# Sample-state and retention stages of a hybrid decoder layer: deeper buffers, operations between engines, another spread of matmul products

## The chip, the core and the metric

The kernel runs on one core of a Trainium2 chip. The engines are called as the profile calls them: PE (matrix multiply; PEld is its weight load), DVE (VectorE), ACT (ScalarE), POOL (GpSimd), SP (SyncE, which here issues only DMAs). POOL issues DMAs too, beside its own arithmetic. The metric is the device time of one launch in microseconds (us). The kernel before took 1690.91 us, the median of three runs from 1685.97 to 1693.16.

## The reference, cut to what matters

One inference step of a one-layer decoder for a prompt of 1024 positions and 8 sample sequences of 4 positions (32 columns), so 1056 columns go through each projection:

```python
xn = rms_norm(x, g_pre_mix); h = xn @ w_in           # 1024 -> 5888 columns
q_a, k_a, v_a, q_r, k_r, v_r, gate_r, gm_a, gm_r = split(h)
o_a = sliding-window attention(q_a, k_a, v_a)         # 8 heads, 128 wide window
# retention, 4 heads, key 128, value 256, chunks of 128 (prompt) or 4 (sample):
scores = (q @ k.T) * dmask;  inner = scores @ v
cross  = (q @ s0) * q_decay
s_new  = gamma**L * s0 + (k * k_decay).T @ v
o_r = head_rms(inner + cross)
mixed = (sigmoid(gm_a) * (o_a @ w_a) + sigmoid(gm_r) * ((silu(gate_r) * o_r) @ w_r)) @ w_o
x = x + rms_norm(mixed);  x = x + rms_norm(conv_ffn(rms_norm(x)))
```

For the samples, `s0` is an input of 8 sequences x 4 heads x 128 x 256 numbers, and `s_new` is an output of the same size.

## The kernel before, in words

**Precision.** A matrix is held as two fp32r tiles, a high part (an ACT copy that rounds) and a low part (source minus high, usually on DVE). The helper `split(hi, lo, src, eng=None)` does both, the low on `eng` or, by default, on DVE. A multiply is three matmuls (lines 255, 256, 257). The helper `ew` (lines 223 and 225) records every elementwise operation: on DVE as a SCALAR_TENSOR_TENSOR at line 223, on POOL as a TENSOR_TENSOR at line 225. So the tiles, not the line, tell such operations apart.

**Products.** Large projections use seven products in place of eight for a 2x2 block multiply. One product is 4 x 3 = 12 matmuls of 128x264. `in_split` loads the raw weights of one pair of 128-column groups of `w_in` (1 MB, two DMAs on SP), forms four sums of 128x512 on DVE and splits seven operands (`w_split`: ACT copy, DVE low). `stream()` is a generator that runs the 16 pairs of this stage, in the order of the list `ORDER`; each of its `yield`s stands behind one product. `adv(n)` runs n products. Pairs 0 to 3 are the retention q and k of heads 0 to 3, pairs 4 to 7 the output gates, 8 to 15 the merge gates. A finished pair is handed to a `post` function: `post_qk` applies the rotary (per half of the columns and per q or k: a DVE shuffle, a POOL multiply by `rcos`, a DVE multiply of `sh` by `rsin`, a POOL add of `sh`; tiles 128x528), `post_gate` a Silu on ACT, `post_ga` a Sigmoid on ACT and a DVE multiply by a tile `zt` that SP loads from `gm_d`.

**Sample stage** (about 298 to 448 us of the profile). `adv(18)` runs, then `for h in range(4): for _ in sample(h): adv(3)`. `sample(h)` prepares a head, then goes in four steps over the eight sequences, two at a time: SP loads their states (`s0`, 128x512, line 1018), `split` makes `s0s` from them, four matmuls with 64 rows add `q @ s0` into `po` (line 1024), two masked keys `kb` are made on DVE (line 1028), two matmuls form `k.T @ v` in `pk` (line 1030), DVE updates `s0` from `pk` (line 1031), and POOL issues its store to `ret_sample` (line 1033). After the head and after each step three products follow in the program.

**Block stage** (about 448 to 704 us). 32 blocks, four heads of eight. `front` makes scores and splits, `middle` the matmuls and the running state (line 1134), `tail` the normalised output times the gate. Per block `adv(2)`, `middle`, `adv(1)`, `tail`, `adv(1)`. `loads(g + 1)` brings the next block: q and k for two blocks at a time (line 1079, SP), v per block (line 1081, POOL). In the tails of blocks 0, 1 and 2 of each head weight sums are made for later stages: `quad_sums` loads two quarters of `w_r` or `w_down` into a `zt` tile (two buffers), four DVE operations follow and a store. `z_sums` in blocks 4 and 7, and `post_ga`, use the same two `zt` buffers. After the last tail the remaining products of the stream run, then the multiply by `w_r` begins (its matmuls write `ps_m`) and with it the merge, until about 840 us.

**What sets the order.** The framework orders the instructions of every engine itself, by a simulated timeline; an engine then runs its list strictly in that order, and each instruction waits in front of its engine for its inputs and for its output buffer. Pools give a name so many buffers (`bufs`); a tile that is asked for when all are taken waits until the oldest is released. PE's accumulators `ps_a` have two buffers in these stages.

## Time and profile before

| what | value |
|---|---|
| runs | 1685.97, 1690.91, 1693.16 us |
| profiled execution, device time | 1688.03 us |
| its span (first to last instruction) | 1686.2 us |
| outside the span | 1.8 us |
| mean granted clock of PE | 0.996 |
| busy in the span: PE, DVE, ACT, POOL | 1629.5, 1269.6, 868.4, 500.9 us |

Busy time counts instructions on the engine; DMA issues are not in it. A wait is put down to the operation whose semaphore came last. A row of grouped instructions gives the busy time of all, the mean of one in ns, and the idle time of the engine just before them with what ended it. A row of a window table gives the length, then for PE, PEld, DVE, ACT and POOL the busy time and, in brackets, the number of instructions, then the granted clock of PE, the busy share of the DMA engines and GB/s.

### The profile page before, as it was taken

What the parts mean: (1) busy time and instruction counts of PE and PEld (TensorE: products, weight loads), DVE (VectorE), ACT (ScalarE), POOL (GpSimd) and SP (SyncE); (2) the same over time, 40 slices, a digit from 0 to 9 for tenths busy, and PEclk for the clock granted to TensorE, in tenths of its full rate; (3) what the DMA queues carried; (4) which work ended last, traced back from release to release, by engine and by line L of the source; (5) the groups of instructions that cost most, each with busy time, mean ns of one, the idle gap of its engine ahead of it and who ended that gap; (6) DMA issues with size and microseconds to landing.
All of it is one profiled execution on the core that took longest, in us unless ns stands there. A gap on an engine that the chain in (4) does not pass through costs nothing.

```text
span 1686.2 us, 32968 instructions
## 1 busy us (share of the span) xinstructions
PE 1629.5 (97%) x12643; PEld 1588.5 (94%) x12643; DVE 1269.6 (75%) x2227; ACT 868.4 (51%) x1942; POOL 500.9 (30%) x714
## 2 busy tenths in 40 slices
PE   8999999888999989999999999999999999999997
PEld 7999989888999989999778999999999999999997
DVE  7887737799586677658757888888888888445476
ACT  6566534434566655564433555555555556444343
POOL 4232420455253443331412122212213323111111
PEclk9999999999999999999999999999999999999999
DMA  7312222445686677596722144454444447866664
GB/s 198 66 45 73 80 65 103 135 130 171 205 256 202 213 252 227 183 298 213 234 94 72 60 145 159 148 163 148 149 146 146 146 151 252 257 182 202 194 184 149
DMA packets 268944, 273.92 MB, mean 162 GB/s; under 512 B 22785, under 2 KB 229921, under 8 KB 268770
## 3 DMA queue, kind: packets, MB, share of 16 engines
q1 hardware_dynamic: 235025, 155.25, 31.7%
q0 software_dynamic: 33760, 116.57, 20.0%
q8 instruction: 99, 1.62, 0.4%
q14 instruction: 60, 0.48, 0.1%
HBM read 184.24 MB, written 87.49 MB: 161 GB/s over the span
## 4 chain that ended last, share of the span: by engine, by line
PE 68%; DVE 11%; DMA 9%; issue 7%; ACT 3%; POOL 1%; SPq 1%; DVEq 0%; POOLq 0%; ACTq 0%
PE ps_m L255 9%; PE ps_m L257 9%; PE ps_m L256 9%; PE ps_t L256 8%; PE ps_t L255 7%; PE ps_t L257 7%; PE ps_mm L255 3%; PE ps_mm L256 3%; PE ps_mm L257 3%; PE ps_q L255 2%; PE ps_q L257 2%; PE ps_q L256 2%; DMA a_in<-a_d 1%; DVE w L223 1%; DVE w_lo L223 1%
## 5 line engine op out<-in xcount | busy, mean ns | idle before, releaser
L255 PE MATMUL ps_q<-xh,w 128*128 128x264 f32 x512 | 148.6, 291 | 7.5 <-DVE pair L925 5.1
L223 DVE SCALAR_TENSOR_TENSOR w_lo<-w_raw,w_hi 128x1024 fp32r<-128x1024 f32 x83 | 104.2, 1261 | 66.0 <-ACT w_hi L228 59.0
L255 PE MATMUL ps_t<-xh,w_hi 128*128 128x264 f32 (+2 forms) x524 | 148.9, 284 | 0.0
L256 PE MATMUL ps_t<-xl,w_hi 128*128 128x264 f32 (+2 forms) x524 | 148.7, 284 | 0.0
L257 PE MATMUL ps_t<-xh,w_lo 128*128 128x264 f32 (+2 forms) x524 | 148.0, 283 | 0.0
L257 PE MATMUL ps_m<-xh,w_lo 128*128 128x264 f32 x512 | 145.6, 285 | 1.2 <-DVE w_lo L223 1.2
L255 PE MATMUL ps_m<-xh,w_hi 128*128 128x264 f32 x512 | 145.9, 285 | 0.2 <-ACT w_hi L228 0.2
L256 PE MATMUL ps_m<-xl,w_hi 128*128 128x264 f32 x512 | 145.5, 284 | 0.0
L256 PE MATMUL ps_q<-xl,w 128*128 128x264 f32 x512 | 145.4, 284 | 0.0
L257 PE MATMUL ps_q<-xh,w 128*128 128x264 f32 x512 | 145.3, 285 | 0.0
L223 DVE SCALAR_TENSOR_TENSOR w<-w_raw,w 128x512 fp32r<-128x512 f32 x152 | 106.0, 701 | 26.1 <-ACT w L329 25.7
L1458 DVE SCALAR_TENSOR_TENSOR c_out<-u_ext,fconst,c_out 128x1024 f32<-128x1024 f32 x96 | 121.8, 1279 | 2.6 <-ACT c_out L1454 0.5
L228 ACT CAST w_hi<-w_raw 128x1024 fp32r<-128x1024 f32 x62 | 65.2, 1052 | 107.1 <-PE ps_t L256 75.3
L329 ACT CAST w<-w_raw 128x512 fp32r<-128x512 f32 x152 | 94.2, 622 | 40.4 <-DVE w_raw L223 25.0
L255 PEld LDWEIGHTS ps_q<-xh,w 128*128 128x128 f32 x512 | 96.3, 188 | 10.0 <-DVE pair L925 7.0
L257 PEld LDWEIGHTS ps_t<-xh,w_lo 128*128 128x128 f32 x524 | 98.7, 188 | 0.0
L256 PEld LDWEIGHTS ps_t<-xl,w_hi 128*128 128x128 f32 x524 | 98.6, 188 | 0.0
L255 PEld LDWEIGHTS ps_t<-xh,w_hi 128*128 128x128 f32 x524 | 98.6, 188 | 0.0
L257 PEld LDWEIGHTS ps_m<-xh,w_lo 128*128 128x128 f32 x512 | 96.3, 188 | 1.7 <-DVE w_lo L223 1.7
L255 PEld LDWEIGHTS ps_m<-xh,w_hi 128*128 128x128 f32 x512 | 96.3, 188 | 0.4 <-ACT w_hi L228 0.4
L256 PEld LDWEIGHTS ps_q<-xl,w 128*128 128x128 f32 x512 | 96.4, 188 | 0.0
L256 PEld LDWEIGHTS ps_m<-xl,w_hi 128*128 128x128 f32 x512 | 96.2, 188 | 0.0
(468 smaller groups left out, 6204.9 us busy)
## 6 DMA issues: line engine op xcount, KB each, us to landing
w_raw<-in_w_up SPq DMA_DIRECT2D x48, 512.0 KB, 4.2
w_raw<-in_w_in SPq DMA_DIRECT2D x42, 512.0 KB, 4.3
w_raw<-s_d SPq DMA_DIRECT2D x60, 256.0 KB, 3.9
t_d<-t POOLq DMA_DIRECT2D x24, 528.0 KB, 4.0
t<-t_d POOLq DMA_DIRECT2D x24, 528.0 KB, 5.1
t<-in_w_down SPq DMA_DIRECT2D x40, 256.0 KB, 4.7
s_d<-t POOLq DMA_DIRECT2D x20, 512.0 KB, 3.8
w_raw<-in_w_down SPq DMA_DIRECT2D x36, 256.0 KB, 4.8
```

The lines of the kernel that those rows point to most:

```text
L223: pinned(V.scalar_tensor_tensor(out=out, in0=in0, scalar=1.0, in1=in1, op0=mult, op1=op))
L228: pinned(S.copy(out=hi, in_=src))
L255: TE.matmul(ps, wh, xh, start=start, stop=False, **kw)
L256: TE.matmul(ps, wh, xl, start=False, stop=False, **kw)
L257: TE.matmul(ps, wl, xh, start=False, stop=stop, **kw)
L329: S.copy(out=t[:, 0:4], in_=src)
L1458: V.scalar_tensor_tensor(out=c[:, NS:], in0=u[:, g, NU + t:NU + t + SEQ], scalar=sc[t], in1=c[:, NS:], op0=mult, op1=add)
```

## The change

- `sample`: the state loads go through `load_s0`, with four buffers in place of two, and are issued two steps ahead (the first two before `adv(18)`). The masked keys `kb` are made by ACT (`S.mul`) and not by DVE. The low part of `s0s` is made by POOL and not by DVE. `r8` and the sample's `o` have one buffer in place of two, and `os8` shares the buffer of `t8`.
- Four products, not three, follow each head start and each step (`adv(4)`).
- Blocks: `qk` is loaded for one block at a time into three buffers, `vt` has four buffers in place of three, both two blocks ahead. The products per block alternate between 3 and 4 (`adv(g % 2)`).
- The weight sums are made in the tails of blocks 0, 2 and 6, no longer 0, 1 and 2.
- `in_split`: the second sum is written over the first (`s1`). `ORDER` puts gate 0 ahead of the q and k of head 3, and the first two merge-gate pairs (8 and 9) one place later.

```diff
-    ORDER = [0, 1, 2, 3, 4, 5, 8, 6, 9, 7, 10, 11, 12, 13, 14, 15]
+    ORDER = [0, 1, 2, 4, 3, 5, 6, 8, 7, 9, 10, 11, 12, 13, 14, 15]
...
-        s1, s2 = [wx["sum"].tile([P, 4, P], F32, name="s%d" % q) for q in range(2)]
+        s1 = wx["sum"].tile([P, 4, P], F32, name="s1")
         yield w_split(a11, V)
         ew(V, s1, a21, a22, add)
         yield w_split(s1, V)
-        ew(V, s2, s1, a11, sub)
-        yield w_split(s2, V)
+        ew(V, s1, s1, a11, sub)
+        yield w_split(s1, V)
         yield w_split(a12, V)
-        ew(V, a12, a12, s2, sub)
+        ew(V, a12, a12, s1, sub)
...
+    s0s_ = {}
+
+    def load_s0(n):
+        if n >= 2 * DB:
+            return
+        h, bb = n // 4, 2 * (n % 4)
+        s0s_[n] = ST("s0", (P, 2, 256), bufs=4)
+        ld.dma_start(out=s0s_[n], in_=I["state_ret"][0, bb:bb + 2, h].rearrange("b k e -> k b e"))
...
-        r8 = ST("r8", (P, 2, P), bufs=2)
+        r8 = ST("r8", (P, 2, P))
...
-            s0 = ST("s0", (P, 2, 256), bufs=2)
-            ld.dma_start(out=s0, in_=I["state_ret"][0, bb:bb + 2, h].rearrange("b k e -> k b e"))
+            s0 = s0s_[(h * DB + bb) // 2]
+            load_s0((h * DB + bb) // 2 + 2)
             s0s = ST("s0s", (P, 2, 2, 256), F32R)
-            split(s0s[:, 0], s0s[:, 1], s0)
+            split(s0s[:, 0], s0s[:, 1], s0, G)
...
-                V.tensor_scalar(out=kb, in0=f32(h8)[:, 1], scalar1=bm[:, bb + b:bb + b + 1],
-                                scalar2=None, op0=mult)
+                S.mul(kb, f32(h8)[:, 1], bm[:, bb + b:bb + b + 1])
...
-        os8 = ST("o", (P, 256), bufs=2)[:NS]
+        os8 = ST("t8", (P, 256))[:NS]
...
+    for n in range(2):
+        load_s0(n)
     adv(18)
     for h in range(4):
         for _ in sample(h):
-            adv(3)
+            adv(4)
...
-    def loads(g):
+    def load_qk(g):
...
-        if tt % 2 == 0:
-            qks[g // 2] = qk2 = ST("qk2", (P, 2, 2 * P), bufs=2)
-            c = NS + P * tt
-            ld.dma_start(out=qk2, in_=qk_d[h].rearrange("i p t -> p i t")[:, :, c:c + 2 * P])
-        vts[g] = ST("vt", (P, 2, 256), F32R, bufs=3)
+        qks[g] = ST("qk", (P, 2, P), bufs=3)
+        ld.dma_start(out=qks[g], in_=qk_d[h].rearrange("i p t -> p i t")[:, :, cols(tt)])
+
+    def load_v(g):
...
+        vts[g] = ST("vt", (P, 2, 256), F32R, bufs=4)
         st.dma_start(out=f32(vts[g][:, 1]), in_=v_d[h, tt])
...
-        if tt < 3:
+        if tt in (0, 2, 6):
             q_ = quarters(ST("zt", (P, T), bufs=2))
-            down_sums(20 + h, q_) if tt == 2 else quad_sums(w_r, r_d, h, 0, tt, q_)
+            down_sums(20 + h, q_) if tt == 6 else quad_sums(w_r, r_d, h, 0, tt // 2, q_)
...
-        loads(g + 1)
+        load_qk(g + 2)
+        load_v(g + 2)
...
         adv(2)
         m = middle(g, *f)
-        adv(1)
+        adv(g % 2)
...
-    adv(len(ORDER) * 14 - 8 - 78 - 4 * NBLK - 1)
+    adv(len(ORDER) * 14 - 8 - 98 - 7 * NBLK // 2 - 1)
```

Two places show how the lists of the engines move. First POOL, in a stretch of sample steps while the rotary of a q and k pair runs (`pair<-pair,rcos` and `pair<-pair,sh` are the rotary; `out_ret_sample` is the store of a step's states; `rs` a reciprocal root). Before:

```order
L225 TENSOR_TENSOR pair<-pair,rcos 128x528
L225 TENSOR_TENSOR pair<-pair,sh 128x528
L1033 DMA out_ret_sample<-s_4346 128x2x256
L826 DMA qk_d<-pair 128x2x528
L225 TENSOR_TENSOR pair<-pair,rcos 128x528
L1033 DMA out_ret_sample<-s_4421 128x2x256
L225 TENSOR_TENSOR pair<-pair,sh 128x528
```

and in the change, over as many steps:

```order
L225 TENSOR_TENSOR s0s<-s_4249,s0s 128x512
L225 TENSOR_TENSOR pair<-pair,sh 128x528
L1037 DMA out_ret_sample<-s_4168 128x2x256
L225 TENSOR_TENSOR pair<-pair,rcos 128x528
L225 TENSOR_TENSOR pair<-pair,sh 128x528
L225 TENSOR_TENSOR s0s<-s_4454,s0s 128x512
L1037 DMA out_ret_sample<-s_4249 128x2x256
L826 DMA qk_d<-pair 128x2x528
```

The lows of the states now stand between the rotary's operations on POOL, one per step, ahead of that step's store.

The second place is DVE in steps of the same kind (`kb` the masked keys, `w` and `w_raw` weights of the products, `s` followed by a number the states or a weight sum, `sh` the rotary). Before:

```order
L1028 TENSOR_SCALAR kb<-h_4656,bm 128x128
L1031 SCALAR_TENSOR_TENSOR s_4715<-s_4715,ps_a 128x512
L1028 TENSOR_SCALAR kb<-h_4656,bm 128x128
L223 SCALAR_TENSOR_TENSOR s0s<-s_4794,s0s 128x512
L223 SCALAR_TENSOR_TENSOR w_4774<-w_raw,w_4774 128x512
L925 TENSOR_TENSOR pair<-ps_q_4664,pair 128x264
L223 SCALAR_TENSOR_TENSOR w_raw<-w_raw,s_4680 128x512
L822 STREAM_SHUFFLE sh<-pair 128x528
```

In the change:

```order
L223 SCALAR_TENSOR_TENSOR sh<-sh,rsin 128x528
L1035 SCALAR_TENSOR_TENSOR s_4168<-s_4168,ps_a 128x512
L223 SCALAR_TENSOR_TENSOR w7x<-w_raw,w7x 128x512
L822 STREAM_SHUFFLE sh<-pair 128x528
L223 SCALAR_TENSOR_TENSOR sh<-sh,rsin 128x528
L1035 SCALAR_TENSOR_TENSOR s_4249<-s_4249,ps_a 128x512
L223 SCALAR_TENSOR_TENSOR s_4603<-w_raw 128x512
```

Between two state updates (line 1031, now 1035) DVE no longer has the masked keys and the low of the states, and has what the products and the rotary need.

More of the change, by code (lines that the diff above doesn't have):

```diff
@@ L852, in trunk @@
     pairs += [(GM0 + m * P, GM0 + m * P + P, post_gm(m)) for m in range(0, KD, 2)]
-    def in_ahead(n):
-        ws = pair_split(pair_weights(w_in, *pairs[n][:2]))
-        return itertools.chain([next(ws) for _ in range(NPRE)], ws)
-    ORDER = [0, 1, 2, 3, 4, 5, 8, 6, 9, 7, 10, 11, 12, 13, 14, 15]
+    ORDER = [0, 1, 2, 4, 3, 5, 6, 8, 7, 9, 10, 11, 12, 13, 14, 15]
     PEND = []
@@ L969, in rep, with finish @@
         return a.rearrange("p (o t) -> p o t", o=1).broadcast_to([P, 4, NS])
-    def finish(po, n, s, h):
+    def finish(po, n, s, h, bufs=2):
         ssq = sml.tile([P, 1], F32, name="ss")[:n]
-        o = ST("o", (P, 256), bufs=2)[:n]
+        o = ST("o", (P, 256), bufs=bufs)[:n]
         S.activation(o, po[:n, :256], AF.Square, accum_out=ssq)
@@ L1034, in sample @@
             yield
-        os8 = ST("o", (P, 256), bufs=2)[:NS]
+        os8 = ST("t8", (P, 256))[:NS]
         S.copy(out=os8, in_=po[NS:2 * NS])
         V.tensor_tensor(out=os8, in0=po[0:NS], in1=os8, op=add)
-        S.copy(out=z8[:, h], in_=turn(pt, finish(os8, NS, 1, h)))
+        S.copy(out=z8[:, h], in_=turn(pt, finish(os8, NS, 1, h, 1)))
+    for n in range(2):
+        load_s0(n)
     adv(18)
@@ L1075, in loads @@
         h, tt = divmod(g, NB)
[L1076 to L1080 removed]
+        qks[g] = ST("qk", (P, 2, P), bufs=3)
+        ld.dma_start(out=qks[g], in_=qk_d[h].rearrange("i p t -> p i t")[:, :, cols(tt)])
+    def load_v(g):
+        if g >= NBLK:
+            return
+        h, tt = divmod(g, NB)
+        vts[g] = ST("vt", (P, 2, 256), F32R, bufs=4)
         st.dma_start(out=f32(vts[g][:, 1]), in_=v_d[h, tt])
@@ L1099, in front @@
         h, tt = divmod(g, NB)
-        q, k = (qks[g // 2][:, i, P * (tt % 2):P * (tt % 2) + P] for i in range(2))
+        q, k = (qks[g][:, i] for i in range(2))
         vt = vts[g]
@@ L1187, in ahead @@
             state["dm"] = mask(g // NB)
-        loads(g + 1)
+        load_qk(g + 2)
+        load_v(g + 2)
         return front(g, state["dm"])
-    loads(0)
+    for g in range(2):
+        load_qk(g)
+        load_v(g)
     coming, behind = ahead(0), None
```

2 lines of the change are left out of this document (1 added, 1 removed).

## The prediction

> **What bounds the kernel now.** I read the page's busy shares first, then a table of windows by stage, then the waits of PE in the two stages that the change touches, and last single instructions.
>
> ```profile
> PE 1629.5 (97%) x12643; PEld 1588.5 (94%) x12643; DVE 1269.6 (75%) x2227; ACT 868.4 (51%) x1942; POOL 500.9 (30%) x714
> 298.00:424.00 126.00, 108.65 (x839) 103.98 (x839) 116.74 (x195) 51.97 (x134) 67.86 (x57) 0.99 0.47 148
> 424.00:448.00 24.00, 21.10 (x172) 20.50 (x171) 13.22 (x28) 10.90 (x24) 4.38 (x6) 1.00 0.61 194
> 448.00:729.00 281.00, 270.44 (x2189) 266.39 (x2190) 201.35 (x509) 168.38 (x459) 116.66 (x190) 0.99 0.71 226
> 729.00:840.00 111.00, 107.84 (x781) 101.23 (x781) 84.85 (x125) 56.00 (x99) 38.00 (x28) 1.00 0.78 240
> 940.00:1200.00 260.00, 260.00 (x2141) 260.00 (x2140) 229.74 (x380) 148.21 (x302) 63.41 (x108) 1.00 0.44 141
> ```
>
> PE is the bound of the whole, and the change adds or removes no matmul, so what can be gained is PE's idle time where the lists differ: 17.35 + 2.90 = 20.3 us in the sample stage (298 to 448), 10.6 us in the blocks and the tail of the stream (448 to 729), 3.2 us in the merge. The last row is a stretch where PE never waits: 260 / 2141 = 0.1214 us per matmul, 1.46 us per product of 12. In the sample stage DVE is busy 116.74 of the first 126 us, 93%; it is nearly the bound there.
>
> ```profile
> PE ps_q L255 <- DVE pair L927: 8.2, 4, 3.0
> PE ps_a L1030 <- DVE kb L1028: 3.5, 5, 1.2
> PE ps_b L1024 <- ACT s0s L228: 2.4, 3, 1.0
> PE ps_q L255 <- ACT pair L902: 2.1, 2, 1.3
> PE ps_q L255 <- DVE pair L925: 1.8, 2, 1.1
> PE ps_b L1024 <- DVE s0s L223: 1.3, 2, 0.8
> PE ps_b L1015 <- DVE h L1010: 1.1, 1, 1.1
> ...
> PE ps_a L1103 <- DVE state L1134: 4.3, 4, 1.4
> PE ps_q L255 <- DVE pair L925: 3.4, 3, 1.8
> PE ps_q L255 <- DVE pair L927: 1.7, 2, 1.0
> ```
>
> The first seven rows are the sample stage, the last three the blocks. Nearly all waits end with an operation of DVE that came late, `pair` L925 and L927 (a PSUM bank is read out) above all.
>
> Why DVE is late shows in single instructions (start, length):
>
> ```profile
> 341.53 1.61 POOL L225 TENSOR_TENSOR pair<-pair,sh 128x528 f32<-128x528 f32 x1 [0.71 <-DVE sh L223]
> ...
> 341.91 1.32 DVE L1028 TENSOR_SCALAR kb<-h,bm 128x128 fp32r<-128x128 f32 x1
> ...
> 343.75 0.27 DVE L1028 TENSOR_SCALAR kb<-h,bm 128x128 fp32r<-128x128 f32 x1
> ...
> L225 POOL TENSOR_TENSOR pair<-pair,sh 128x528 f32<-128x528 f32 x16 | 25.2, 1576 | 13.3 <-DVE sh L223 13.0
> L225 POOL TENSOR_TENSOR pair<-pair,rcos 128x528 f32<-128x528 f32 x16 | 25.0, 1563 | 26.8 <-DVE sh L822 23.6 <-DVE t L1006 1.6 <-DVE kb L1028 1.4
> ...
> L1028 DVE TENSOR_SCALAR kb<-h,bm 128x128 fp32r<-128x128 f32 x32 | 17.2, 549 | 0.1
> L223 DVE SCALAR_TENSOR_TENSOR w<-w_raw,w 128x512 fp32r<-128x512 f32 x22 | 17.1, 783 | 1.6 <-ACT w L329 1.6
> L223 DVE SCALAR_TENSOR_TENSOR sh<-sh,rsin 128x528 f32<-128x528 f32 x16 | 16.9, 1056 | 0.7 <-DMA rsin<-in_rsin 0.5
> L223 DVE SCALAR_TENSOR_TENSOR s0s<-s,s0s 128x512 fp32r<-128x512 f32 x16 | 11.8, 734 | 4.4 <-ACT s0s L228 4.3
> L925 DVE TENSOR_TENSOR pair<-ps_q,pair 128x264 f32<-128x264 f32 x11 | 4.7, 424 | 0.0
> L223 DVE SCALAR_TENSOR_TENSOR s<-s,w_raw 128x512 f32<-128x512 f32 x6 | 4.1, 683 | 0.0
> ```
>
> A masked key takes 0.27 us alone and 1.32 us when it comes while POOL runs a rotary operation: it ends 0.09 us after POOL's. [...] Against the undisturbed 0.27 and 0.68 us (0.70 for 528 columns), the three dearest rows lost 17.2 - 8.6 = 8.6, 17.1 - 15.0 = 2.1 and 16.9 - 11.2 = 5.7 us: 16.4 us against 50.2 us of rotary on POOL, a third.
>
> **The change part by part, sample stage.**
>
> Masked keys to ACT: the 3.5 us that PE waits for `kb` go, and DVE loses 17.2 us of work. ACT gains 32 small operations, some 0.3 us each (an estimate from the next fence's 128x128 casts), 10 us on an engine busy 62.9 of 150. Bounds: 2 to 3.5 us of gain.
>
> ```profile
> L228 ACT CAST sT<-s 128x128 fp32r<-128x128 f32 x32 | 9.6, 299 | 24.3 <-DVE s L1106 24.3
> ...
> ACT s0s L228 <- DMA s<-in_state_ret: 21.9, 10, 3.8
> ...
> SPq L1018 <- DMA out_ret_sample<-s: 70.8, 13, 14.4
> ```
>
> State loads two steps ahead: SP stood 70.8 us in front of these loads because the buffer's store had not landed, and ACT stood 21.9 us in front of the cast with PSUM copies queued behind it. With four buffers the load for step n+2 needs only the store of step n-2. The 2.4 us that PE waits for the ACT part of `s0s` go. Bounds: 1 to 2.4.
>
> Lateness of DVE: the other waits of PE here, 8.2 + 2.1 + 1.8 + 1.3 + 1.1 = 14.5 us. There is a price on top:
>
> ```profile
> 447.97 0.39 PE L255 MATMUL ps_q<-ex,w7x 128*128 128x264 f32 x1 [2.90 <-DVE pair L927]
> ...
> 316.00:320.00 4.00, 1.56 (x9) 1.57 (x10) 3.96 (x5) 1.16 (x3) 2.39 (x3) 0.89 0.00 0
> 320.00:330.00 10.00, 10.00 (x75) 10.00 (x74) 7.71 (x13) 3.07 (x9) 5.55 (x5) 0.88 0.55 167
> ...
> 448.00:452.00 4.00, 4.00 (x21) 4.00 (x22) 1.72 (x4) 3.77 (x9) 3.55 (x7) 0.60 0.43 134
> ```
>
> After each of two gaps of nearly 3 us the granted clock falls, to a mean of 0.88 and 0.60, which loses 4 x 0.11 + 10 x 0.12 = 1.6 and 4 x 0.40 = 1.6 us more. [...]
>
> How much of these 17.7 us goes hangs on DVE's load. It was 130.0 us in 150. Out go 17.2 (keys) and 11.8 (lows). In come 20 products, moved here from the blocks: half a low and two sevenths of a sum each (0.68 us a piece), 0.53, and two sevenths of an output add (0.42), 0.12, so 13.0 us. And POOL gets 16 lows of about 1.57 x 512 / 528 = 1.52 us, 24.3 us; at one third DVE loses 8.1 us to them. DVE then has 122 us to do in 150 + 20 x 1.46 = 179 us less the gain, some 167: 73%, where it was 87%. I keep half, a gain of 8.9 us; bounds nothing (the waits come in bursts) and all 17.7.
>
> Lows on POOL: PE's four `q @ s0` matmuls now hang on POOL's list. In a step with rotary POOL has 4 x 8 / 14 = 2.3 rotary operations (3.6 us), a low (1.5), a store (0.74, by the next row) and its share of others, about 6.2 us in a step in which PE needs 4 x 1.46 + 6 x 0.12 = 6.6 us. That is close, and it ends when the rotaries do.
>
> ```profile
> L1033 POOL DMA_DIRECT2D out_ret_sample<-s x16 | 11.8, 739 | 25.4 <-DVE s L1031 15.7 <-DVE kb L1028 9.8
> ```
>
> Bounds for 16 steps: no wait, or each waits one rotary operation, 16 x 1.57 = 25 us. The lows stand ahead of their use by some products in most steps, so I take 0.25 us a step, 4 us.
>
> [...]
>
> Single buffers for `r8`, `o` and the shared `t8`: at a head's start only, with products to cover; 0, at worst 4 heads x 1 us.
>
> **Blocks.** Their waits are DVE's lateness again, here from transfers:
>
> ```profile
> ACT vt L228 <- DMA vt<-v_d: 22.6, 10, 6.5
> ...
> DVE pair L223 <- DMA zt<-gm_d: 4.2, 3, 1.4
> DVE zt L223 <- DMA zt<-in_w_r_proj: 4.0, 4, 1.8
> ```
>
> Loads two blocks ahead cover the 22.6 us of ACT; weight sums in blocks 0, 2 and 6 leave the two `zt` buffers more time, against 8.2 us that DVE waits for two of their loads. A block has 3.5 products, 5.1 us, in place of 5.8, so less cover: DVE's 201 us less 13 over 281 less 29 is 75%, where it was 72%. Of the 9.4 us in the three rows I take half, 4.7; bounds 9 of gain and 5 of loss.
>
> **Merge.** After the last tail four products fewer run, 5.8 us.
>
> ```profile
> 720.97 1.22 DVE L223 SCALAR_TENSOR_TENSOR w_lo<-w_raw,w_hi 128x1024 fp32r<-128x1024 f32 x1 [0.41 <-ACT w_hi L228]
> ...
> 729.20 0.28 PE L255 MATMUL ps_m<-xh,w_hi 128*128 128x264 f32 x1
> ```
>
> The weights of the next stage are ready at 722.2, 7.0 us ahead. That covers 5.8 just so: 0.5 us of loss, bounds 0 and 3. From 840 us on nothing changes.
>
> **Sum** on the profiled execution of 1688.0: -3.5 - 2.4 - 8.9 + 4.0 - 4.7 + 0.5 = -15.0, which makes 1673. The profiled execution lies 2.9 us under the median of the runs; I add about half of that: **1675 us**.
>
> **Rivals.**
>
> [...] The lows on POOL hold DVE off as much as DVE was freed, and thinner blocks give nothing: -3.5 - 2.4 + 4.0 + 0.5 = -1.4, 1687. For it: DVE lost a third of POOL's time already. Against it: 29 us of DVE work leave.
>
> *POOL's list becomes the bound (slower).* Place: the `q @ s0` matmuls of each step, behind the rotary in POOL's list. If each step waits a rotary operation, 25 us, and DVE's lateness stays as it is: 1688.0 - 5.9 + 25 - 4.7 + 0.5 = 1703. It beats the gains of the other parts (5.9 + 8.9 + 4.7 = 19.5) from 1.2 us of wait per step on. For it: 6.2 of 6.6 us. Against it: it holds for rotary steps only, some 12 of 16. [...]
>
> *DVE's lateness goes altogether (faster still).* -5.9 - 17.7 - 9.4 + 2 = -31, 1657. It needs a DVE at 73% that is never late; in the blocks, at 72%, it was.
>
> That the change does not do what it says I leave out: the order has one low per step on POOL and none on DVE.
>
> **How the numbers follow.** Forecast (1665 to 1682) 0.55, no change 0.22, slower 0.12, faster still 0.11. Half a percent is 8.5 us, about what runs that spread over 7 us can tell from no change; faster begins under 1682.5. So faster 0.66, same 0.22, slower 0.12. The range 1660 to 1691 takes in the no-change case and the half of the faster one, and leaves out most of the slower one; the forecast's own range is 1665 to 1682.
>
> **What would show it.** Sample stage: PE's waits for `kb` and for the ACT part of `s0s` gone, those on `pair` L925 and L927 about halved, no drop of the granted clock; ACT's 21.9 us and SP's 70.8 us gone. PE waits on POOL for `s0s` under 6 us in sum say the cost of the lows is right; over 15 says the slower rival. DVE's two-input operations keep means above 0.68 us where POOL runs. Blocks: ACT's wait for `vt` and DVE's for `zt` nearly gone, PE idle 10.6 to about 6 us. Merge: first `ps_m` matmul without a wait of over 1 us. The prediction is wrong if PE's idle time in the sample stage stays above 16 us, or if the blocks lose what it gains.

## The result, and the profile after

The changed kernel takes 1694.95 us (median of 20 runs, 1689.92 to 1697.43); the kernel before, run beside it, 1688.76 (20 runs, 1684.36 to 1695.91). The ratio is 1.0028, 95% interval 1.0017 to 1.0038: no change by the half percent of the prediction, but on the slower side, and 20 us above the 1675 that was forecast. By the ratio the change costs 4.7 us, by the two medians 6.2; below, a difference in us that stands without two times beside it is the ratio's.

First the busy times of the changed kernel's page (us, share of the span, instructions):

```profile
PE 1636.2 (97%) x12643; PEld 1596.2 (94%) x12643; DVE 1266.0 (75%) x2179; ACT 878.0 (52%) x1972; POOL 514.4 (30%) x730
```

Then its windows by stage. The stages moved a little: the sample stage ends at about 468 us, the blocks at 731.7, the merge at 850.3 us. Columns as before: window, length, busy time of PE, PE's weight loads, DVE, ACT, POOL, granted clock, DMA share, GB/s.

```profile
298.00:424.00 126.00, 112.86 (x889) 109.75 (x888) 102.44 (x151) 61.47 (x154) 78.04 (x63) 0.99 0.45 146
424.00:468.00 44.00, 42.80 (x346) 41.80 (x345) 29.70 (x48) 25.76 (x64) 20.90 (x21) 1.00 0.51 164
468.00:732.00 264.00, 248.13 (x1972) 243.91 (x1971) 190.46 (x487) 151.51 (x425) 114.08 (x187) 0.97 0.72 228
732.00:850.30 118.30, 111.89 (x780) 104.68 (x780) 91.78 (x129) 60.24 (x106) 36.17 (x31) 0.96 0.79 244
940.00:1200.00 260.00, 260.00 (x2141) 260.00 (x2140) 229.64 (x378) 149.68 (x308) 60.20 (x113) 1.00 0.42 136
```

PE's idle time in the sample stage fell from 20.3 to 13.1 + 1.2 = 14.3 us. In the blocks it rose from 10.6 to 15.9, in the merge from 3.2 to 6.4; a wait of 1.8 us just behind the merge, at 841.5 us of the kernel before, is gone. The granted clock, which was 0.99 and 1.00 in blocks and merge, is now 0.97 and 0.96. The last row is the same as before.

The waits of PE in the changed kernel, in the sample stage (first five rows) and in the blocks (next five; rows of under 1 us are left out but for POOL's) (line, what it waited for, us in total, times, longest):

```profile
PE ps_q L255 <- DVE pair L921: 5.3, 5, 2.3
PE ps_q L255 <- DVE pair L923: 3.2, 4, 1.8
PE ps_b L979 <- ACT o L973: 2.2, 1, 2.2
PE ps_q L255 <- ACT pair L898: 1.9, 2, 1.3
PE ps_b L1029 <- POOL s0s L225: 0.8, 2, 0.4
...
PE ps_a L255 <- DVE kt L1120: 3.8, 2, 3.2
PE ps_a L1112 <- DVE state L1143: 3.2, 3, 1.8
PE ps_q L255 <- DVE pair L923: 2.8, 3, 1.1
PE ps_b L255 <- DVE z L1162: 2.4, 2, 2.1
PE ps_a L1112 <- DMA qk<-qk_d: 2.1, 1, 2.1
```

The waits for `kb` and for ACT's part of `s0s` are gone, and POOL's lows are late by 0.8 us in all. New in the blocks are single long waits: `kt` 3.2 us, `z` 2.1, `qk` 2.1.

What a long wait brings shows in narrow windows around two of them, in the changed kernel:

```profile
473.00:476.40 3.40, 3.40 (x31) 3.40 (x30) 0.69 (x1) 2.15 (x4) 0.00 (x0) 1.00 0.77 243
476.40:479.90 3.50, 1.49 (x13) 1.27 (x11) 0.00 (x0) 0.00 (x0) 0.75 (x1) 0.99 1.05 294
479.90:483.30 3.40, 3.27 (x15) 3.30 (x16) 2.01 (x5) 2.20 (x9) 0.91 (x2) 0.50 0.82 258
...
510.50:514.00 3.50, 1.49 (x13) 1.29 (x11) 0.64 (x2) 0.97 (x4) 0.67 (x2) 1.00 0.77 274
514.00:520.80 6.80, 5.61 (x25) 5.61 (x26) 6.75 (x22) 2.54 (x7) 3.50 (x6) 0.50 0.27 84
```

In 476.4 to 479.9 PE stands 2 us; in the next 3.4 us it is busy, at half clock, and gets through 15 matmuls where 31 fit. The wait of 3.2 us near 512 is followed by 6.8 us at half clock. Between 298 and 850 us the changed kernel has six such stretches at half clock (called half-speed stretches below), starting at 374.0, 479.9, 514.0, 619.8, 776.8 and 831.4 us; the kernel before has two, at 319.1 and 448.8.

That gives an account of the span. Add PE's idle time between 298 and 850 us to half of PE's busy time inside half-speed stretches: 35.8 + 3.4 = 39.2 us before, 36.6 + 12.6 = 49.3 after. Over the profiles of all twenty kernels of this study the span less this sum is 1642.5 to 1648.3 us, while the spans run from 1677.0 to 1699.7. So PE's idle time hardly changed; it came in fewer and longer pieces (42 gaps before, 36 after). Gaps of over 1.77 us (the number is explained at the end) are four before and eight after. Of the 10.1 us by which the sum grew, 9.2 are the clock. The span itself grew by 7.6 us: the rest of it got 2.5 us shorter, and why is not known.

### The profile page after: what moved, and what is told of

It is laid out like the page before. It is cut to its first block, busy times and chain, and to the rows that moved or that the text cites. A ratio compares the mean times of both kernels' runs of the same rounds, so it can differ in the third digit from the quotient of the medians.

```text
span 1693.8 us, 33019 instructions
## 1 busy us (share of the span) xinstructions
PE 1636.2 (97%) x12643; PEld 1596.2 (94%) x12643; DVE 1266.0 (75%) x2179; ACT 878.0 (52%) x1972; POOL 514.4 (30%) x730
## 3 DMA queue, kind: packets, MB, share of 16 engines
q8 instruction: 99, 1.62, 0.4%
## 4 chain that ended last, share of the span: by engine, by line
PE 74%; DVE 8%; DMA 7%; issue 6%; ACT 2%; POOL 1%; SPq 0%; DVEq 0%; POOLq 0%; ACTq 0%
PE ps_m L256 9%; PE ps_m L257 9%; PE ps_m L255 9%; PE ps_t L256 7%; PE ps_t L255 7%; PE ps_t L257 7%; PE ps_q L255 3%; PE ps_q L257 3%; PE ps_q L256 3%; PE ps_mm L255 3%; PE ps_mm L256 3%; PE ps_mm L257 3%; DMA w_raw<-in_w_in 2%; DVE w L223 1%; PE ps_a L255 1%
## 5 line engine op out<-in xcount | busy, mean ns | idle before, releaser
L255 PE MATMUL ps_q<-xh,w 128*128 128x264 f32 x512 | 150.7, 295 | 8.2 <-DVE pair L921 6.0
L257 PE MATMUL ps_q<-xh,w 128*128 128x264 f32 x512 | 147.0, 288 | 0.0
L223 DVE SCALAR_TENSOR_TENSOR w<-w_raw,w 128x512 fp32r<-128x512 f32 x152 | 112.0, 741 | 24.2 <-ACT w L329 23.8
L255 PEld LDWEIGHTS ps_q<-xh,w 128*128 128x128 f32 x512 | 97.7, 191 | 10.7 <-DVE pair L921 7.6
L257 PEld LDWEIGHTS ps_q<-xh,w 128*128 128x128 f32 x512 | 97.8, 191 | 0.0
```

The lines of the kernel that those rows point to most:

```text
L223: pinned(V.scalar_tensor_tensor(out=out, in0=in0, scalar=1.0, in1=in1, op0=mult, op1=op))
L255: TE.matmul(ps, wh, xh, start=start, stop=False, **kw)
L257: TE.matmul(ps, wl, xh, start=False, stop=stop, **kw)
```

## The experiments

Theories at the outset. A: the blocks lose what the sample stage gains, since the loads two blocks ahead stand at the head of SP's list. B: the lows on POOL hold DVE off as much as they free it. C: any edit makes the scheduler lay out another order, and the few long gaps that an order happens to have decide. D: the pace (3.5 products a block) or the spread weight sums.

### One part of the change undone

`a_oldloads` puts back the block loads:

```diff
-        qks[g] = ST("qk", (P, 2, P), bufs=3)
+        if tt % 2 == 0:
+            qks[g // 2] = qk2 = ST("qk2", (P, 2, 2 * P), bufs=2)
...
-        vts[g] = ST("vt", (P, 2, 256), F32R, bufs=4)
+        vts[g] = ST("vt", (P, 2, 256), F32R, bufs=3)
...
-        load_qk(g + 2)
-        load_v(g + 2)
+        loads(g + 1)
```

> The changed kernel with only the block loads put back (q and k in pairs of blocks, one block ahead, three buffers of v). Theory A (the blocks lose what the sample stage gains, because the loads two blocks ahead stand at the head of SP's list, 70.0 us against 28.3, and w_raw, zt and q,k land late behind them): SP's wait for a q,k buffer falls below 35 us, PE's idle time in the blocks from 15.9 to 10 or less, at most two half-speed stretches there instead of three, time 1683 to 1688. Theories B (the lows on POOL), C (any new order of instructions scatters the time) and D (the thinner pace of products): SP's wait falls as well, but PE's idle in the blocks stays at 14 to 17 and the time at 1692 to 1698.

`a_lowsdve` puts the lows of the sample states back on DVE:

```diff
-            split(s0s[:, 0], s0s[:, 1], s0, G)
+            split(s0s[:, 0], s0s[:, 1], s0)
```

> The changed kernel with only the lows of the sample states back on DVE. Theory B (POOL's 23.4 us of lows hold DVE off by as much as they free it): DVE's mean for s<-s and w<-w_raw in the sample stage goes back from 1.58 and 0.98 us towards 0.68 and 0.78, PE's idle there stays at 14 us or falls, time 1687 to 1691. Theory A: the sample stage's idle time grows by 2 to 4 us with the lows' work on DVE, the blocks stay as they are, time 1695 to 1700.

`a_oldpace` puts back the pace and the list of pairs:

```diff
-    ORDER = [0, 1, 2, 4, 3, 5, 6, 8, 7, 9, 10, 11, 12, 13, 14, 15]
+    ORDER = [0, 1, 2, 3, 4, 5, 8, 6, 9, 7, 10, 11, 12, 13, 14, 15]
-            adv(4)
+            adv(3)
-        adv(g % 2)
+        adv(1)
```

> The changed kernel with only the pace and the order of the products put back (3 a sample step, 4 a block, the old list of pairs). Theory D (3.5 products a block are too few to cover a block's chain): PE's idle in the blocks falls from 15.9 to about 11, idle in the sample stage rises by 2 to 3 for want of the fourth product, time 1688 to 1691. Theory A: SP's list still stands for the q,k buffers in the blocks, their idle stays at 14 to 17, and with the sample stage worse the time is 1696 to 1700.

`a_oldsums` puts the weight sums back to blocks 0, 1 and 2:

```diff
-        if tt in (0, 2, 6):
+        if tt < 3:
```

> The changed kernel with only the weight sums put back to the first three blocks of a head. If spreading them hurts (theory D's other half: a sum in block 6 now meets z_sums of block 7 and the next head's mask and gate): PE's idle in the blocks falls by 3 or more, time 1688 to 1691. Theory A: the blocks stay within 2 us of 15.9, or grow with the bunched sums, time 1694 to 1699.

Measured, as ratio to the kernel before: `a_oldloads` 0.9988 (0.9976 to 1.0000), `a_lowsdve` 0.9986 (0.9973 to 1.0000), `a_oldpace` 1.0044 (1.0029 to 1.0059), `a_oldsums` 1.0041 (1.0029 to 1.0053). Inside the change, pace and sums are not what hurts (D falls): undoing either leaves the time at or above that of the change, 1696.51 and 1695.14 us, in the ranges that A gave for them. Undoing the loads or the lows each takes 7 us off, as A and B said. But where they take it off fits neither. In `a_oldloads` SP's wait for a q,k buffer fell only to 44.7 us, and the blocks' idle time to 13.4 us, not 10. In `a_lowsdve` the gain is not in the sample stage, whose code was edited (idle 17.7 us there, above the change's 14.3), but in the blocks, whose code is that of the change: idle 8.3 us against 15.9.

What the lows on POOL do to DVE shows in the window of the sample stage. This is the row of `a_lowsdve`:

```profile
298.00:470.00 172.00, 154.27 (x1238) 150.48 (x1237) 131.98 (x214) 87.25 (x218) 78.59 (x73) 1.00 0.47 153
```

And this is the row of the changed kernel:

```profile
298.00:470.00 172.00, 157.66 (x1250) 153.55 (x1249) 133.68 (x200) 88.86 (x220) 100.94 (x87) 0.99 0.47 151
```

With the 14 more instructions that DVE runs in this window when it keeps the lows, it is busy 131.98 us; with the lows on POOL, 133.68. POOL's 22 us more bought DVE nothing. Groups of instructions show where the time went. First the lows in the changed kernel, on POOL (busy us, mean ns of one):

```profile
L225 POOL TENSOR_TENSOR s0s<-s,s0s 128x512 fp32r<-128x512 f32 x16 | 23.4, 1460 | 8.1 <-ACT s0s L228 4.6 <-issue 3.4
```

Then three groups of DVE in the same stage of the changed kernel, whose means were 783, 1056 and 683 ns before:

```profile
L223 DVE SCALAR_TENSOR_TENSOR w<-w_raw,w 128x512 fp32r<-128x512 f32 x28 | 27.1, 984 | 3.5 <-ACT w L329 3.4
L223 DVE SCALAR_TENSOR_TENSOR sh<-sh,rsin 128x528 f32<-128x528 f32 x16 | 18.8, 1174 | 1.3 <-DMA rsin<-in_rsin 1.1
L223 DVE SCALAR_TENSOR_TENSOR s<-s,w_raw 128x512 f32<-128x512 f32 x7 | 11.1, 1579 | 0.2
```

Not all of that rise is the lows' doing. In `a_lowsdve`, whose sample stage differs from the change only by them:

```profile
L223 DVE SCALAR_TENSOR_TENSOR sh<-sh,rsin 128x528 f32<-128x528 f32 x16 | 18.1, 1128 | 1.0 <-DMA rsin<-in_rsin 0.8
L223 DVE SCALAR_TENSOR_TENSOR s0s<-s,s0s 128x512 fp32r<-128x512 f32 x16 | 14.2, 889 | 2.9 <-ACT s0s L228 2.9
L223 DVE SCALAR_TENSOR_TENSOR s<-s,w_raw 128x512 f32<-128x512 f32 x7 | 6.2, 887 | 0.1
```

Up to 468 us `w<-w_raw,w` takes 24.4 us there, 27 of 914 ns. So the three groups take 48.7 us with the lows on DVE and 57.0 with the lows on POOL (one `w` more): 8.3 of the 14.2 us that the lows cost DVE come back in these three alone.

### The order alone, both parts, and single parts on the kernel before

`n_phase` gives the half product of a block to even blocks in place of odd ones, `adv(1 - g % 2)` for `adv(g % 2)`: the same instructions in another order.

> The changed kernel with the half product of a block given to even blocks in place of odd ones: the same instructions, loads and buffers, only another order. Theories A (the loads two blocks ahead) and B (the lows on POOL) both hold that an edit that touches neither leaves the time where it is: 1693 to 1697, PE's idle in the blocks 14 to 17. Theory C (each order leaves its own few gaps of 2 to 3 us in the blocks and the merge, and what decides is which of them the clock punishes): idle in the blocks anywhere from 8 to 17, time anywhere from 1684 to 1700, most likely outside 1692 to 1697.

`a_both` has the edits of `a_oldloads` and `a_lowsdve`.

> The changed kernel with both the old block loads and the lows on DVE. Each alone took about 9 us off the changed kernel. If A and B are two separate losses, they add: 1675 to 1679, with PE's idle in the blocks at 8 or less. If C is right, each was one draw of an order, and they do not add: 1682 to 1692.

`s_all` has the edits of `a_oldloads`, `a_oldpace` and `a_oldsums`, so that only the sample stage's part of the change stays.

> The changed kernel with loads, pace, list of pairs and weight sums of the blocks all as before: what stays is the sample stage's part (state loads two steps ahead, masked keys on ACT, lows on POOL) and the single sum tile. By the prediction's terms (-3.5 for the masked keys, -2.4 for the state loads, +4.0 for the lows, some 2 to 4 of DVE's lateness): 1682 to 1687. Theory B: 1688 to 1692, no gain in the sample stage. Theory C: idle in the sample stage falls by about 4 us from 20.3, but the time lies anywhere from 1683 to 1698.

`b_kb` is the kernel before with one edit:

```diff
-                V.tensor_scalar(out=kb, in0=f32(h8)[:, 1], scalar1=bm[:, bb + b:bb + b + 1],
-                                scalar2=None, op0=mult)
+                S.mul(kb, f32(h8)[:, 1], bm[:, bb + b:bb + b + 1])
```

> The kernel before with only the masked keys moved to ACT. The prediction's term: PE's waits for kb go, 3.5 us, time 1683 to 1686. Theory C: the waits for kb go as well, but the order of everything behind moves, and blocks and merge take or give up to 8 us of it: 1681 to 1694.

Measured: `n_phase` 1.0010 (0.9993 to 1.0028), `a_both` 0.9987 (0.9974 to 1.0001), `s_all` 1.0060 (1.0041 to 1.0078), `b_kb` 0.9986 (0.9972 to 1.0000). The two undone parts do not add: 0.9988 and 0.9986 alone, 0.9987 together. The masked keys alone gain 2.4 us, and alone bring PE's idle time in the sample stage from 20.2 to 14.8 us, as low as the whole change. The sample stage's part without the new pace is the slowest kernel so far: 1697.74 us, outside what the prediction's terms (1682 to 1687) and theory B (1688 to 1692) gave for it. A as first put falls (with the old loads, `s_all` is at 1.0060).

Theory C's ranges are wide, and a time that lies in them says little. Its direct test, `n_phase`, is not clear: its interval and the change's (1.0017 to 1.0038) overlap. What speaks for C so far is that the parts do not add.

### The lows again, the sample stage without them, and the merge

`s_nolow` is `s_all` with the lows on DVE; `b_lows` is the kernel before with `split(..., s0, G)`; `nl_phase` has the edits of `n_phase` and `a_lowsdve`.

> The sample stage's part alone (blocks' loads, pace, list of pairs and sums as before), now with the lows of the sample states on DVE: what stays is state loads two steps ahead, masked keys on ACT and the single sum tile. Theory B in its present form (the lows on POOL are what turns the change: with them on POOL the six kernels run so far took 0.9988 to 1.0060 of the kernel before and left 13 to 18 us of idle in PE's blocks, with them on DVE three took 0.9986, with 8 to 14): 0.997 to 1.000, 1682 to 1687, where the same kernel with the lows on POOL took 1697.7. Theory C (every order is its own draw): 0.997 to 1.006.

> The kernel before with only the lows of the sample states moved to POOL. The prediction's term is +4.0 us for their latency and a gain on DVE's side. Theory B: DVE's busy time in 298 to 470 us stays within 3 us of 143.9 though 16 instructions of 0.73 us are gone, PE waits for POOL's lows, and the time is 1.002 to 1.006, 1690 to 1698. Theory C: 0.998 to 1.006. If the lows were harmless: 0.997 to 1.000.

> The changed kernel with the lows on DVE and the half product given to even blocks. Theory B: the lows decide and not the order, 0.997 to 1.000 as with the lows on DVE alone (0.9986). Theory C: the same instructions in another order, 0.997 to 1.006; with the lows on POOL the same step moved the time from 1.0028 to 1.0010.

`al_merge` is `a_lowsdve` with one more line, for the gap near the end of the merge:

```diff
-        eng = G if m < 4 else V
+        eng = G if m < 4 and not half else V
```

> The changed kernel with the lows on DVE, and with the second-half merges of rows 0 to 3 on DVE in place of POOL. In four of the kernels PE stands 3.0 to 3.2 us for the last transposed low weight (w_loT) near 815 to 829 us, where DVE's lows of Gr take 1.5 us each beside POOL's merges and 0.42 us without them, and the clock falls right behind. If POOL's work is what holds DVE there: those lows take 0.42 us, PE's gap falls below 1.5 us, no half-speed stretch follows, time 3 to 5 us under the 1684.2 of the lows on DVE alone, 1678 to 1682. If the gap is the late weight's transfer: it stays at 3 us and the time at 1683 to 1687.

Measured: `s_nolow` 1.0065 (1.0051 to 1.0080), `b_lows` 1.0039 (1.0025 to 1.0052), `nl_phase` 0.9983 (0.9969 to 0.9997), `al_merge` 0.9964 (0.9947 to 0.9981). The lows on POOL alone cost 6.6 us on the kernel before, and there too DVE does not get lighter. The same window of the kernel before:

```profile
298.00:470.00 172.00, 151.75 (x1175) 146.29 (x1175) 143.89 (x258) 76.76 (x193) 82.40 (x80) 0.98 0.53 169
```

And that of `b_lows`:

```profile
298.00:470.00 172.00, 152.25 (x1151) 146.43 (x1150) 144.72 (x228) 74.86 (x183) 100.50 (x91) 0.96 0.49 159
```

B holds for DVE's load and, on three of five pairs of kernels, for the time (1.0039 against 1, 1.0028 against 0.9986, 1.0010 against 0.9983, where the intervals overlap). Two pairs go against it as a full explanation: `s_all` and `s_nolow` are equally slow, which was outside the ranges of both theories for `s_nolow`, and `a_oldloads` and `a_both` are equally fast (0.9988 and 0.9987). So something else is in the sample stage's part. And with the lows on DVE the order of the half products changes nothing: `nl_phase` 0.9983, `a_lowsdve` 0.9986.

Where `b_lows` lost its time is in its profile: from 298 to 850 us PE's idle time is 36.0 us, against 35.8 before, but there are four half-speed stretches in place of two, all in the sample stage.

The merge experiment came out as the prediction's no-change rival (1687 us) has it, that POOL's work holds DVE off: DVE's lows of `Gr` took about 1.5 us each beside POOL's merges and 0.42 us without them. DVE's timeline in the changed kernel (start, length), before PE's gap of 3.13 us that ends with `w_loT`:

```profile
826.40 4.48 DVE L223 SCALAR_TENSOR_TENSOR xl<-Gr,xh 128x264 fp32r<-128x264 f32 x3
830.80 1.21 DVE L223 SCALAR_TENSOR_TENSOR w_loT<-w_raw,w_hiT 128x1024 fp32r<-128x1024 f32 x1
```

POOL's timeline of the same stretch:

```profile
825.91 1.76 POOL L1246 TENSOR_TENSOR Gr<-Gr,g_in 128x528 f32<-128x528 f32 x1 [0.52 <-ACT g_in L1243]
827.75 1.40 POOL L1247 TENSOR_TENSOR Gr<-Gr,a_in 128x528 f32<-128x528 f32 x1
829.10 1.49 POOL L1246 TENSOR_TENSOR Gr<-Gr,g_in 128x528 f32<-128x528 f32 x1
```

Three lows of `Gr` take 4.48 us, one after another as POOL's three operations end; the last ends at 830.9, POOL's at 830.6. In `al_merge` two of the same lows take 0.77 us, though DVE now does these merges as well (its DVE timeline):

```profile
818.69 0.77 DVE L223 SCALAR_TENSOR_TENSOR xl<-Gr,xh 128x264 fp32r<-128x264 f32 x2
819.38 0.70 DVE L1246 TENSOR_TENSOR Gr<-Gr,g_in 128x528 f32<-128x528 f32 x1
820.00 1.22 DVE L223 SCALAR_TENSOR_TENSOR w_loT<-w_raw,w_hiT 128x1024 fp32r<-128x1024 f32 x1
```

PE's wait for `w_loT` is gone there, and so is the half-speed stretch behind it.

### The other single parts, and the cure on the kernel before

`b_s1` is the kernel before with one sum tile in place of two, `b_s0x3` the kernel before with the state loads two steps ahead (three buffers, and `r8`, `o`, `t8` shared as in the change), `b_pace` with the new pace and list of pairs; `bk_merge` is `b_kb` with the merge line of `al_merge`.

> The kernel before with only one tile for the sums of a weight pair in place of two: the second sum overwrites the first, so it waits for both halves of the first one's split, and each next pair waits for the tile. If this is what the sample stage's part loses: 1.004 to 1.008, 1694 to 1701, with more of PE's idle time on weights in the blocks. If it is harmless, as the prediction took it without a term: 0.998 to 1.001.

> The kernel before with only the state loads two steps ahead (three buffers, r8, o and t8 shared as in the change). The prediction's term: PE's waits for the ACT part of the state split go, 2.4 us, 0.998 to 0.999. If the loads ahead are what hurts (they stand in SP's list ahead of the weight loads and wait there for a store): 1.003 to 1.008, and SP's wait for the state stores stays above 40 us.

> The kernel before with only the new pace and list of pairs (4 products a sample step, 3.5 a block). The prediction's term: PE's idle in the sample stage falls by 3 to 9 us from 20.3 as 20 more products cover DVE, blocks lose up to 5: 0.995 to 1.000. If thin blocks are what costs: idle in the blocks rises by 5 or more from 10.6, 1.001 to 1.005.

> The kernel before with masked keys on ACT and the second-half merges of rows 0 to 3 on DVE. The first alone took 0.9986; its PE gaps at 818 and 821 us are 1.34 and 1.58 us and bring no half-speed stretch, so the merge's cure is worth 1 to 3 us here: 0.996 to 0.998, 1681 to 1684. If it was worth the 2.4 us between al_merge and a_lowsdve only by the draw of the order: 0.998 to 1.000.

Measured: `b_s1` 1.0038 (1.0026 to 1.0050), `b_s0x3` 1.0081 (1.0069 to 1.0093), `b_pace` 1.0044 (1.0024 to 1.0064), `bk_merge` 0.9974 (0.9963 to 0.9986). Of the five single parts that were tried on the kernel before, only the masked keys gain; the block loads and the weight sums were not tried alone on it. Together the five would make 1.019 if they added; the whole change is at 1.0028. What a part costs depends on the rest, which is what theory C says, though parts that share engines and waits need not add in any case.

`b_s1`, for which the prediction had no term, costs 6 us (4.4 by the medians), and not by idle time, which is 33.5 us from 298 to 850 against 35.8 before: five half-speed stretches, four of them in the sample stage, lose 11.1 us where 3.4 were lost. `b_pace` brings PE's idle time in 298 to 470 only from 20.2 to 19.4 us, where a fall of 3 to 9 was expected. The cure of the merge gains 0.0019, 0.0022 and 0.0012 in its three pairs (`a_merge`, which follows below, `al_merge`, `bk_merge`, each against its kernel without it); in each pair the intervals overlap, but all go the same way.

`b_s0x3` is the clearest case. At its own place PE's wait for ACT's part of `s0s` went, as the prediction had it, and SP's wait for the state stores fell from 70.8 to 60.1 us. In the sample stage it won little: PE's idle time to 470 us is 22.3, against 20.2 before, and 2.9 of it are already the wait for the first block. PE waits 2.6 us there for a head's normalised output, whose reciprocal root stands on POOL behind two rotary operations of 4.01 and 1.62 us, and a half-speed stretch follows at 405.3; whether the shared single buffers have a part in that was not tried. The most was lost at the start of the blocks. PE's waits of `b_s0x3` from 440 to 520 us:

```profile
PE ps_a L1114 <- DVE state L1145: 3.1, 1, 3.1
PE ps_a L1114 <- DMA qk<-qk_d: 2.9, 1, 2.9
```

The q,k of the first block are late there as in the change, 2.9 us, and two of its four half-speed stretches follow these two waits. That led to the last question: why are they late? For `b_s0x3` SP's list gives an answer. In the kernel before it issues the first q,k loads at 438.5 us. Here they come at 456.9, while PE is ready for them only 8 us later than before. They stand behind a `w_raw` load whose buffer SP waits for (SP's waits from 430 to 490 us):

```profile
SPq L340 <- DVE w L223: 10.1, 1, 10.1
```

### The place of one load in one list

SP's own timeline at the end of the sample stage, in the changed kernel:

```profile
453.30 0.47 SPq L1099 DMA_DIRECT2D z<-gr_d  x1
470.81 0.37 SPq L340 DMA_DIRECT2D w_raw<-in_w_in  x1
471.27 3.16 SPq L1083 DMA_DIRECT2D qk<-qk_d  x2
```

The same place in `a_lowsdve`:

```profile
455.05 0.47 SPq L1099 DMA_DIRECT2D z<-gr_d  x1
455.57 1.82 SPq L1083 DMA_DIRECT2D qk<-qk_d  x3
```

And the longest wait of SP from 452 to 472 us in the changed kernel:

```profile
SPq L340 <- DVE w L223: 17.0, 1, 17.0
```

In the change a `w_raw` load stands ahead of the first q,k loads and waits 17.0 us for its buffer; they are issued at 471.3, and PE waits for them at 477.9. In `a_lowsdve` the scheduler put them ahead of it: 455.6, and PE does not wait. So an edit in the sample stage moved two loads past one. `a_qkst` tests just this: the first two blocks' q,k go on POOL's list.

```diff
-        ld.dma_start(out=qks[g], in_=qk_d[h].rearrange("i p t -> p i t")[:, :, cols(tt)])
+        (st if g < 2 else ld).dma_start(out=qks[g], in_=qk_d[h].rearrange("i p t -> p i t")[:, :, cols(tt)])
```

> The changed kernel with the q,k loads of the first two blocks on POOL's list in place of SP's, where they stood behind a w_raw load that waits 17.0 us. If that place is a cause: PE's gap at the first block's front (2.14 us at 478 us) falls below 0.5 us and the half-speed stretch at 479.9 goes, 2 to 4 us, 1689 to 1693, ratio 1.000 to 1.002. If q,k are late for another reason: the gap stays and the ratio is 1.002 to 1.004.

`a_merge` is the change with the merge line of `al_merge` alone.

> The changed kernel with the second-half merges of rows 0 to 3 on DVE in place of POOL, lows of the sample states still on POOL. The gap of 3.13 us at 829 us and the half-speed stretch behind it (1.7 to 3.4 us lost) go: ratio 1.000 to 1.001, 1687 to 1690. If what al_merge gained was the draw of the order: 1.002 to 1.004.

Measured: `a_qkst` 0.9972 (0.9957 to 0.9987), `a_merge` 1.0009 (0.9996 to 1.0022). Against the change these are 9 and 3 us; the second is what was expected (its interval and the change's overlap), the first more than twice as much. Up to 468 us `a_qkst` runs as the change does, lows on POOL and all. Its profile is of the fastest of its 12 runs (1678.75 us, the median is 1681.80), so it flatters a little. Its windows:

```profile
298.00:424.00 126.00, 113.05 (x891) 109.86 (x890) 102.95 (x152) 61.92 (x155) 78.34 (x63) 0.99 0.46 147
424.00:468.00 44.00, 42.67 (x347) 41.77 (x347) 29.67 (x47) 25.47 (x64) 20.93 (x21) 1.00 0.50 161
468.00:717.60 249.60, 240.07 (x1968) 237.26 (x1967) 189.85 (x486) 151.36 (x424) 115.69 (x189) 1.00 0.75 241
717.60:833.40 115.80, 110.94 (x783) 104.10 (x782) 89.84 (x127) 60.00 (x105) 35.77 (x30) 0.97 0.80 250
```

The sample stage is that of the change to within 0.2 us of PE busy time. PE then runs 1968 matmuls of the blocks in 249.6 us, where the change needs 264 for 1972; idle 9.5 us against 15.9, granted clock 1.00 against 0.97. POOL issues the two loads at 469.1 and 470.4 us, only 2.2 us ahead of SP in the change, just what PE had waited. The waits of PE in its blocks:

```profile
PE ps_q L255 <- DVE pair L923: 3.5, 3, 1.2
PE ps_a L1112 <- DVE state L1143: 2.0, 3, 1.2
PE ps_b L255 <- ACT sT L228: 1.4, 1, 1.4
PE ps_a L255 <- DVE kt L1120: 1.2, 1, 1.2
```

None is longer than 1.4 us. With the wait for q,k the later long ones went too: `kt` (3.2 us in the change) and `z` (2.1). In the change `kt` was late because DVE stood 5.18 us for a weight load in front of it (DVE's timeline, changed kernel):

```profile
507.90 0.28 DVE L1115 TENSOR_TENSOR s<-ps_a,dm 128x128 f32<-128x128 f32 x1
513.36 0.71 DVE L223 SCALAR_TENSOR_TENSOR s<-w_raw 128x512 f32<-128x512 f32 x1 [5.18 <-DMA w_raw<-in_w_in]
...
514.80 0.34 DVE L1120 SCALAR_TENSOR_TENSOR kt<-ps_a,kdec,kt 128x128 fp32r<-128x128 f32 x1
```

A part stays open. Moving two loads to another list also made the scheduler lay out the blocks anew, so the 9 us are the loads' place and the new order together; the two cannot be had apart with these kernels. And a late first q,k is not the whole of theory C: of the twenty kernels the nine in which PE waits 2.0 to 2.9 us for it have ratios from 0.9988 to 1.0081, mean 1.0036, the eleven without from 0.9964 to 1.0044, mean 0.9998. `b_lows`, `b_s1` and `b_pace` are slow without it.

`al_merge`, at 0.9964, is the fastest kernel found, level with `a_qkst` within the intervals: 1681.78 us against 1687.44 for the kernel before run beside it. It is the change less the lows on POOL, with four merges more on DVE.

## Why the prediction was wrong

Told in PE's idle time and half-speed stretches, from the two profiles: the sample stage, with the stretch that follows its last gap before, gained 7.6 us where 10.8 were forecast, the blocks lost 11.4 where a gain of 4.7 was forecast, the merge lost 8.1 where 0.5 was forecast, and 1.8 us were gained behind it. So the blocks' term failed first: what it left out is where their first q,k loads come to stand in SP's list. Moving these two loads, with the new order of the blocks that came with it, took back 9 us.

- **Masked keys, -3.5:** right in what goes away. PE's waits for `kb` are gone, and alone the edit took 2.4 us (0.0 to 4.7 by the interval).
- **State loads, -2.4:** the mechanism was seen at its place (ACT's wait for the loads fell from 21.9 to 3.6 us, SP's from 70.8 to 47.0, PE's for ACT's `s0s` to nothing), the sign of the whole was not: alone, with three buffers in place of four, the edit costs 0.8%. The step that failed is "With four buffers the load for step n+2 needs only the store of step n-2", which counted what the load waits for, not where the other loads come to stand in SP's list: in `b_s0x3` the first q,k loads are issued 18 us later than before.
- **DVE's lateness, -8.9:** failed at "DVE then has 122 us to do". DVE was busy 102.44 + 29.70 = 132.1 us, 78% of the stage and not 73%. The lows, put down with 11.8 us of relief less 8.1, brought none: DVE was 1.7 us busier with them on POOL (the change against `a_lowsdve`), where 3.7 us of relief were counted, which is 5.4 of the 10 us missed. The other half is not traced. The waits on the two `pair` lines fell from 10.0 to 8.5 us and were not halved. One drop of the clock stayed, at 374.0. Alone, the new pace with its 20 more products took 0.9 us off PE's idle time. This is the no-change rival's mechanism, and for DVE it was right.
- **Lows on POOL, +4.0:** PE's waits on POOL are 0.8 us, so neither that term nor the slower rival's place was right; the lows came in time. POOL's list shows at another place, the 2.2 us for ACT's `o`: its reciprocal root started on POOL at 366.6 us, behind a rotary operation of 3.30 us. The lows' price is in what they do to DVE and the clock: 6.6 us alone on the kernel before.
- **The single sum tile of `in_split`:** no term, and no reason given for none. Alone it costs 4 to 6 us, in half-speed stretches.
- The sample stage as a whole gained 6 us of idle time and one half-speed stretch. The line "wrong if PE's idle time in the sample stage stays above 16 us" did not apply; its other half, "if the blocks lose what it gains", did.
- **Blocks, -4.7:** wrong sign, and the largest error: idle time +5.3 us, and three half-speed stretches (479.9, 514.0, 619.8) where only the one behind the sample stage's last gap had been. "Loads two blocks ahead cover the 22.6 us of ACT" brought them to 14.5 only; DVE's waits for two `zt` loads rose from 8.2 to 14.0. The bound "5 of loss" took waits as costing their length; the clock behind them came on top, and no term named the position of the first q,k loads.
- **Merge, +0.5:** the cover at its start held (no wait of over 1 us for the first `ps_m`). The merge lost 3 us of idle time and two half-speed stretches at places that the prediction did not look at. The one at 831.4 follows the late `w_loT`; the one at 776.8 follows waits of 1.6 and 0.8 us for `w_hi` and `w_lo`, each shorter than 1.77 us, together 2.4 us. In `a_merge` the wait for `w_loT` and its half-speed stretch are gone, and the 3 us that it gains fit, within the overlap of the intervals.
- In general: the sum priced each edit at its own place. Of the gains that were tried alone, only the masked keys' had the right sign. That the order laid out anew is the reason was seen at one place, the first q,k loads; for the other parts it is argued and not shown, and the two tests of the order alone (`n_phase`, `nl_phase`) moved nothing clear of noise.

## What to carry to other kernels

Where a scheduler sets the order, compare the two orders at the entry of each stage that follows the edited one: look for a load that has come to stand behind one that waits long. Weigh PE's gaps one by one rather than by their sum, since the long ones were paid a second time in clock here (12.6 us of the changed kernel's 49.3). Before moving elementwise work to POOL to relieve DVE, look at what DVE's own operations take beside POOL's (here a median of 1.53 us against 0.70 for `sh<-sh,rsin`).

## What was not expected of the hardware

**In these traces the half-speed stretches lie on a grid of 3.41 us.** The half-speed stretches of an execution, at a granted clock of 0.50, start at multiples of 3.413 us from each other: in the change 374.0, 479.9, 514.0, 619.8, 776.8 and 831.4 are 31, 10, 31, 46 and 16 such steps apart. If one lays windows of this length over the twenty profiles from 250 to 900 us, each by its own half-speed stretches, leaving out windows that are themselves at half speed, all 64 windows with 1.85 us or more of PE idle time are followed by one at half clock; of the 3629 with less than 1.70 us three are; the line is put between the two, at 1.77 us, 52% of the window, which is an estimate. The grid's place differs between profiles. Six kernels that share the sample stage (the change, `a_oldloads`, `a_oldsums`, `n_phase`, `a_qkst`, `a_merge`) have the same gap of 2.21 to 2.24 us near 366 us; in three of them a half-speed stretch follows it, in three none does. That this is a source of the spread of 7 us between runs of one program is inferred, since each program has one profile. By this line a gap g between 1.77 and 3.41 us is caught in (3.41 + g - 2 x 1.77) / 3.41 of all positions, 0.62 for 2.24 us; for the four long gaps before and the eight after that is an estimate of 2.7 and 5.2 stretches of 1.7 us, 4.3 us of difference on average, beside the 4.7 to 6.2 measured.

**DVE got no lighter by what POOL took over.** Lows on POOL left DVE's busy time where it was, 133.7 against 132.0 us in the change and 144.7 against 143.9 in the kernel before. Not every DVE operation took longer beside POOL. Over five of the profiles (both kernels, `a_lowsdve`, `b_lows`, `b_kb`; 298 to 850 us), the median of `sh<-sh,rsin`, with two inputs in SBUF, is 0.70 us where no POOL arithmetic runs beside it and 1.53 where at least 0.25 us of it do. The shuffle, with one input, takes 0.75 and 0.76 us (seven cases beside POOL), and `pair<-ps_q,pair`, which reads PSUM, 0.42 in both. So inputs in SBUF are not enough to make an operation slower beside POOL: the shuffle's input lies there too.
